# A two-layer hybrid decoder step: the order of three mixer branches and their gates

## The chip, the core and the metric

One core of a Trainium2 chip runs the whole program in one launch. The metric is the device time of one execution in microseconds (us); lower is better. Five engines run side by side, each through its own instructions in order: TensorE (PE, matrix products, with PEld for its weight loads), VectorE (DVE), ScalarE (ACT), GpSimd (POOL) and SyncE (SP, which issues most DMAs). Semaphores between them make an instruction wait for its inputs and for the buffers it overwrites.

## The reference

Two layers are applied to a prompt of 256 tokens and to 8 sample sequences of 4 tokens each, 288 columns in all, with a model width of 1024. Each layer has a mixer block, cross attention over 256 memory tokens, and a convolutional feed-forward network. The change is inside the mixer block, which is, cut to its core:

```python
h = rmsnorm(x, p['norm_mix_g'])
(q_a, k_a, v_a, x_b, y_b, q_c, k_c, v_c, r_c, a_c, g_a, g_b, g_c) = jnp.split(h @ p['w_in'], offs, axis=-1)
o_a = swa_banded(q, k, v, sink)  or  swa_step(q, k, v, k_buf, v_buf, sink)    # local attention
xc, _ = causal_dwconv(x_b, ...); hr, _ = rg_lru(xc, ...); o_b = gelu(y_b) * hr  # recurrence
o, _ = gla(q_c, k_c, v_c, log_alpha, s0); o_c = rmsnorm(o) * silu(r_c)          # linear attention
merged = (sigmoid(g_a) * (o_a @ p['w_branch_a'])
          + sigmoid(g_b) * (o_b @ p['w_branch_b'])
          + sigmoid(g_c) * (o_c @ p['w_branch_c']))
return merged @ p['w_out'], states
```

The sum over the three branches may be taken in any order.

## The kernel before

Activations lie transposed: 128 features on the partitions, 288 columns (256 of the prompt, 32 of the samples) along the free axis. Each large product takes 128x128 weight tiles against 128x288 activations, in three products of reduced-precision halves: `mm3` (L213 to L215) multiplies weight high by activation high, weight high by activation low, weight low by activation high. A weight tile of 128x1024 arrives by SP in a buffer `wst` (4 of them), ACT rounds it to `whi` (L142) and DVE subtracts to get `wlo` (L143), in 3 buffers each. A gate, an input projection or an output takes pairs of output tiles into one of two PSUM tiles `mm`; 24 products make an output tile of a gate, 48 a pair. Small steps (transposes, scores, sums over partitions) use four PSUM tiles `sm` and plain fp32 operands. Activation splits for a product are `split` (L226 to L228): ACT rounds to the high half (L227), DVE subtracts for the low half (L228).

The large products are written out in order. The small work of a layer runs in generators, called chains: `swa` (local attention), `lru` (recurrence), `gla` (linear attention), `mem_load` with `mem_rms` (the norm of the memory tokens), the norms and others. After each pair of k-steps, `proj` calls `tick`, which advances every chain whose next step is ready by an estimate: `account` adds up the time of every instruction (for an fp32 product `n / 600` us for n columns, scaled down for partial rows and columns), and a chain's `ready` is the estimated end of its last step plus 0.3 us plus whatever the generator yields. So a step's place between the large products on PE is fixed when the program is built. PE keeps the written order; the order on ACT, DVE, POOL and SP is set by a scheduler from priorities, with weights and PSUM reads put ahead.

In `swa` the prompt's blocks come first, and then the sample steps: scores of the cached keys (L643), a masked maximum on DVE (L650), exponentials on ACT (L655, L657), normalising on DVE (L659 to L666), transposes on PE (L671, L672), copies on ACT and DVE (L676, L677), the products with the values (L681, L685), a copy on ACT (L689), transposes on PE (L693), copies on ACT (L699), and the split of the sample columns, after which the branch's input `oh`, `ol` is whole. In `lru` the gates of the recurrence are eight fp32 products of 128x312 (L736), each read by a sigmoid on ACT (L737); then the chain yields until `swa` is done, and goes on with exponentials, hyperbolic tangents (L743, L744), a square root (L752), three wide passes on DVE (L747, L750, L754), a scan (L763) and a product with the gelu of the other half.

`gate(x)` makes four gate pairs of branch x (sigmoid on ACT, L1443); `branch(x)` first finishes the chain of that branch, then takes four weight tiles, multiplies each pair by its gate (DVE, L1461) and adds it to the accumulator. Branch 0 is local attention, 1 the recurrence, 2 linear attention. The order in a layer is: gates 0 and 1, branch 0, three pairs of gate 2, half of branch 1, the start of the memory chain, the last pair of gate 2, the rest of branch 1, branch 2, and then the output product `wout`, which reads the split of the accumulator that the last branch makes.

Of the kernel before, what the change touches and what calls it, by code (L numbers as in the profile page):

```python
# [19 lines left out]
KD = D // P  # L20
# [46 lines left out]
def trunk(ctx: ExitStack, tc: tile.TileContext, a: dict):  # L67
    nc = tc.nc
    V, A, PE, G = nc.vector, nc.scalar, nc.tensor, nc.gpsimd
# [78 lines left out]
    active = {}  # L148

    def account(i):  # L150

        if not hasattr(i, "engine") or not i.outs or i.opcode == "DMACopy":
            return
        e, n = str(i.engine), 1
        for _, c in i.outs[0].ap[1:]:
            n *= c
        if i.opcode == "Matmult":
            rows, cols = i.ins[0].ap[0][1], 1
            for _, c in i.ins[1].ap[1:]:
                cols *= c  # L160
            if i.ins[0].dtype == F32R:
                c = n / 2400 + 0.012
            elif getattr(i, "is_transpose", False):
                c = 0.109
            else:
                c = n / 600 * min(1.0, -(-rows // 32) / 4) * min(1.0, -(-cols // 32) / 4)
            est["pe"] += c
            if est["cur"] is not None:
                est["cur"] = max(est["cur"], est["pe"])
            return  # L170
        c = {"EngineType.DVE": 0.09 + n / 970, "EngineType.Activation": 0.12 + n / 1200}.get(e, 0.15 + n / 600)
        f = str(getattr(i, "func", "")).split(".")[-1]
        if i.opcode == "Activation" and f in TABLES and est["table"] not in TABLES[f]:
            est["table"] = TABLES[f][0]
            c += 1.28
        cur = est["cur"] if est["cur"] is not None and est["serial"] else est["pe"]
        t = est["busy"][e] = max(est["busy"].get(e, 0.0), cur) + c
        if est["cur"] is not None and not (est["serial"] and e == "EngineType.Pool"):
            est["cur"] = max(est["cur"], t + 0.1)
# [300 lines left out]
    def swa(l, got, Q, KV):  # L480
# [24 lines left out]
        for kv in range(2):  # L505
            rows = slice(kv * 64, kv * 64 + 64)
# [13 lines left out]

        yield
        pq, pg = flip(ss, 2, P), psm()
# [36 lines left out]
        for blk in range(2):  # L559
# [9 lines left out]
            for j0 in range(0, 4, hb):  # L569

                pscore = [psm(), psm()]
                for j in range(j0, j0 + hb):
                    for kv in range(2):
                        rows = slice(kv * 64, kv * 64 + 64)
# [43 lines left out]
            for kb in range(blk + 1):  # L618
                for kv in range(2):
                    rows = slice(kv * 64, kv * 64 + 64)  # L620
# [14 lines left out]
        for kv in range(2):  # L635
            rows = slice(kv * 64, kv * 64 + 64)
            G.tensor_copy(qblk[rows, :, kv, :, :], Q[rows, :, NP_:T].rearrange("p j (b s) -> p b j s", s=NS))
        yield
        pscore = psm()
# [9 lines left out]
        for g in range(2):  # L649
            V.tensor_tensor_reduce(out=pt[:, g, :], in0=pscore[:, g * 132 : g * 132 + 132], in1=cc("ms"),  # L650
                                   scale=rqs[:, g : g + 1], scalar=-3e38, op0=ALU.add, op1=ALU.max, accum_out=mx[:, g : g + 1])
        yield
        sink = prm[:, l, C_SKS : C_SKS + 1]
        V.tensor_scalar(mx, mx, sink, -1.0, ALU.max, ALU.mult)
        A.activation(es, mx, AF.Exp, bias=sink)  # L655
        for g in range(2):
            A.activation(pt[:, g, :], pt[:, g, :], AF.Exp, bias=mx[:, g : g + 1], accum_out=den[:, g : g + 1])  # L657
        yield
        V.tensor_add(den, den, es)  # L659
# [5 lines left out]
        for g in range(2):  # L665
            V.tensor_mul(pn[:, g], pt[:, g, P : P + NS].unsqueeze(1).to_broadcast([P, NB, NS]),  # L666
                         mb[:, g].unsqueeze(2).to_broadcast([P, NB, NS]))
        yield
        ptr = psm()
        for g in range(2):  # L670
            PE.transpose(ptr[:, g * P : (g + 1) * P], pt[:, g, :P], ident)  # L671
            PE.transpose(ptr[:32, (2 + g) * P : (3 + g) * P], pn[:, g].rearrange("p b s -> p (b s)"), ident)  # L672
        yield
        ptt = m1(2 * P)
        ptn = m1(2 * P)[:32]
        A.copy(ptt, ptr[:, : 2 * P])  # L676
        V.tensor_copy(ptn, ptr[:32, 2 * P : 4 * P])  # L677
        yield
        po = psm()
# [3 lines left out]
        for b in range(NB):  # L683
            r, g = 32 * (b % 4), b // 4
            PE.matmul(po[r : r + 32, g * P : (g + 1) * P], ptt[:, b * 32 : b * 32 + 32], vc[:, b, :], start=False, stop=True,  # L685
                      skip_group_check=True)
        yield
        ot = m1(2 * P)
        A.copy(ot, po[:, : 2 * P])  # L689
        yield  # L690
        po = psm()
        for g in range(2):
            PE.transpose(po[:, g * P : (g + 1) * P], ot[:, g * P : (g + 1) * P], ident)  # L693
        yield
        os = m1(P).rearrange("p (j t) -> p j t", j=4)
# [13 lines left out]
    def lru(l, got, xb, gy):  # L709
# [23 lines left out]
        for t in range(4):  # L733
            for g, (dst, c) in enumerate(((r, C_LBA), (ig, C_LBX))):
                pg = psm()
                PE.matmul(pg[:, :WO], wax[:, g * 4 + t, :], xc[:, t], start=True, stop=True)  # L736
                A.activation(dst[:, t], pg[:, :WO], AF.Sigmoid, bias=prm[:, l, c + t : c + t + 1])  # L737
            yield
        while not active["swa"].done:
            yield  # L740
# [284 lines left out]
    def mem_rms(sqs):  # L1025

        if sqs:
# [4 lines left out]
            A.copy(ss, pss[:, :NP_])  # L1032
            yield
            pt = flip(ss, 2, P)
# [315 lines left out]
    def mixers(l):  # L1350
# [84 lines left out]
        gates, acc = {}, {}  # L1435
# [13 lines left out]
        def branch(x, ms=range(0, KD, 2)):  # L1449
            oh, ol = chains[("swa", "lru", "gla")[x]].finish()  # L1450
            for m in ms:
# [8 lines left out]
                with tc.high_priority(AHEAD):  # L1460
                    V.tensor_mul(g, g, pm[:, :, :T])  # L1461
                if x:
                    (G if x == 1 or m < KD - 4 else V).tensor_add(acc[m], acc[m], g)  # L1463
                else:
                    acc[m] = g
                if x == 2:
                    w = slice(m % 4, m % 4 + 2)
                    split(bh[m // 4][:, w], bl[m // 4][:, w], acc[m])

        gate(0)  # L1470
        gate(1)
        branch(0)
        gate(2, (0, 2, 4))
        branch(1, (0, 2))
        mh = [s5v(4, NP_, F32R), s5v(4, NP_, F32R)]
        ml = [s5v(4, NP_, F32R), s5v(4, NP_, F32R)]
        mem = active["mem"] = Chain(mem_load(l, mh, ml))
        gate(2, (6,))
        branch(1, (4, 6))
        branch(2)  # L1480
        kcs = [load_kc(l, b) for b in range(NB)]
# [196 lines left out]
```

## Time and profile before

| | us |
|---|---|
| median of three runs | 1140.0 (1137.69 to 1142.15) |
| the profiled execution | 1141.05 |
| its span, from the first to the last instruction | 1139.1 |
| PE busy | 1107.9 (97%) |
| DVE busy | 794.3 (70%) |
| ACT busy | 629.8 (55%) |
| POOL busy | 252.4 (22%) |

A busy PE is not a PE at its peak: ends of matrix products are modelled, and a product at the lower clock counts as busy all the while. So the table is read together with two other views: who made PE wait, and the clock that was granted in each stretch. The stretches of which the prediction speaks lie near 40, 178 to 197 and 261 us in layer 0, and near 741 to 764 us in layer 1.

### The profile page before, as it was taken

The page shows a single profiled execution, that of the slowest core. Times are in us where ns is not written, and L with a number is a line of the kernel's source. Part 1 is how long each engine was busy: PE and PEld are TensorE (multiplying, and loading weights), DVE is VectorE, ACT ScalarE, POOL GpSimd, SP SyncE. Part 2 cuts the span into 40 slices and gives each one's busy share as a digit, 9 for nine tenths or more (in the row PEclk, how much of TensorE's full clock was granted, in tenths as well). Part 3 has the DMA queues.
Part 4 walks back from the last instruction along what each step waited for, and adds up shares of the span by engine and source line. Part 5 has one row for each costly group of instructions (what it writes and reads, how often), then busy time and mean ns, then how long its engine had stood idle before and what let it go on. Part 6 is the DMA issues. An engine that isn't in the chain of part 4 may idle for free. (4 is left out here: it accounts for less than half of the span.)

```text
span 1139.1 us, 22360 instructions
## 1 busy us (share of the span) xinstructions
PE 1107.9 (97%) x8846; PEld 1061.3 (93%) x8846; DVE 794.3 (70%) x1454; ACT 629.8 (55%) x971; POOL 252.4 (22%) x426
## 2 busy tenths in 40 slices
PE   9999997999999999999999999979999999999998
PEld 8898986999988999999999989869999899999998
DVE  6876866777765887885458769566776668878743
ACT  6545777535455656654346476864354456566532
POOL 1220101031111455550022100010311014555400
PEclk9999998999999999999999999989999999999999
DMA  8753453567466555556555435445675544455662
GB/s 279 266 181 115 152 179 116 187 201 242 150 221 234 148 167 161 155 162 197 172 170 180 138 103 178 160 141 166 203 242 166 187 142 150 167 160 158 184 193 84
DMA packets 62663, 198.11 MB, mean 174 GB/s; under 512 B 7960, under 2 KB 11768, under 8 KB 62560
## 3 DMA queue, kind: packets, MB, share of 16 engines
q1 hardware_dynamic: 59536, 188.55, 52.0%
q0 software_dynamic: 2880, 8.15, 1.9%
q8 instruction: 69, 1.13, 0.4%
q14 instruction: 34, 0.28, 0.1%
q10 hardware_dynamic: 144, 0.00, 0.0%
HBM read 187.35 MB, written 8.95 MB: 172 GB/s over the span
## 5 line engine op out<-in xcount | busy, mean ns | idle before, releaser
L142 ACT CAST whi<-wst 128x1024 fp32r<-128x1024 f32 (+1 forms) x302 | 312.5, 1036 | 302.1 <-PE mm L214 239.6
L143 DVE TENSOR_TENSOR wlo<-wst,whi 128x1024 fp32r<-128x1024 f32 (+1 forms) x302 | 373.6, 1238 | 143.1 <-ACT whi L142 141.5
L213 PE MATMUL mm<-xh,whi 128*128 128x288 f32 x1488 | 448.4, 301 | 0.0
L214 PE MATMUL mm<-xl,whi 128*128 128x288 f32 x1488 | 440.4, 296 | 1.0 <-DVE xl L264 1.0
L215 PE MATMUL mm<-xh,wlo 128*128 128x288 f32 x1488 | 439.8, 296 | 0.0
L213 PEld LDWEIGHTS mm<-xh,whi 128*128 128x128 f32 x1488 | 280.8, 189 | 12.0 <-issue 9.1
L214 PEld LDWEIGHTS mm<-xl,whi 128*128 128x128 f32 x1488 | 281.0, 189 | 2.6 <-DVE xl L264 1.9
L215 PEld LDWEIGHTS mm<-xh,wlo 128*128 128x128 f32 x1488 | 280.6, 189 | 0.4
L213 PE MATMUL mm<-s,whi 128*128 128x288 f32 (+1 forms) x756 | 226.3, 299 | 8.3 <-ACT s L227 7.4
L214 PE MATMUL mm<-s,whi 128*128 128x288 f32 (+1 forms) x756 | 225.5, 298 | 4.9 <-DVE s L228 4.9
L215 PE MATMUL mm<-s,wlo 128*128 128x288 f32 (+1 forms) x756 | 224.7, 297 | 0.0
L213 PEld LDWEIGHTS mm<-s,whi 128*128 128x128 f32 x756 | 144.8, 192 | 10.7 <-ACT s L227 7.9
L214 PEld LDWEIGHTS mm<-s,whi 128*128 128x128 f32 x756 | 145.0, 192 | 6.4 <-DVE s L228 6.3
L215 PEld LDWEIGHTS mm<-s,wlo 128*128 128x128 f32 x756 | 144.7, 191 | 0.6
L1329 DVE SCALAR_TENSOR_TENSOR y<-u,prm,y 128x304 f32<-128x304 f32 x176 | 83.6, 529 | 0.2
L1333 POOL TENSOR_TENSOR m<-y 128x256 f32<-128x256 f32 x44 | 61.0, 1386 | 70.3 <-ACT y L1330 61.3
L227 ACT CAST s<-m 128x288 fp32r<-128x288 f32 (+1 forms) x46 | 19.6, 426 | 73.7 <-POOL m L1334 73.7
L1327 ACT ACTIVATE y<-u,prm 128x304 f32<-128x304 f32 x88 | 51.9, 635 | 12.8 <-DVE u L1320 12.8
L228 DVE TENSOR_TENSOR s<-m,s 128x288 fp32r<-128x288 f32 (+1 forms) x46 | 20.7, 449 | 47.3 <-ACT s L227 47.3
L269 POOL TENSOR_TENSOR s<-s 128x288 f32<-128x288 f32 x20 | 17.7, 885 | 141.9 <-ACT s L268 141.9
L1313 POOL COPY u<-s 128x32 f32<-128x32 f32 x44 | 44.4, 1011 | 0.0
L1463 POOL TENSOR_TENSOR g<-g,g 128x576 f32<-128x576 f32 x12 | 20.9, 1738 | 79.9 <-DVE g L1461 79.9
(392 smaller groups left out, 1273.9 us busy)
## 6 DMA issues: line engine op xcount, KB each, us to landing
wst<-in_win SPq DMA_DIRECT2D x98, 512.0 KB, 3.5
wst<-in_up SPq DMA_DIRECT2D x88, 512.0 KB, 3.5
wst<-in_down SPq DMA_DIRECT2D x32, 512.0 KB, 3.7
wst<-in_wbr SPq DMA_DIRECT2D x24, 512.0 KB, 3.5
s<-in_mk SPq DMA_DIRECT2D x16, 512.0 KB, 5.6
wst<-in_wout SPq DMA_DIRECT2D x16, 512.0 KB, 4.0
wst<-in_down SPq DMA_DIRECT2D x16, 384.0 KB, 3.2
g<-in_mv SPq DMA_DIRECT2D x16, 256.0 KB, 3.3
```

The source lines that it names most:

```text
L142: A.copy(hi[:, :n], st[:, :n])
L143: (E or V).tensor_sub(lo[:, :n], st[:, :n], hi[:, :n].bitcast(F32))
L213: PE.matmul(out, wh, bh, start=first, stop=False)
L214: PE.matmul(out, wh, bl, start=False, stop=False)
L215: PE.matmul(out, wl, bh, start=False, stop=last)
L227: A.copy(hi, src)
L228: V.tensor_sub(lo, src, hi.bitcast(F32))
L1313: G.tensor_copy(us[:, :, :, 0:2], fhist[:, 2 * c : 2 * c + 2])
L1327: A.activation(y[:, i, :WFO], u[:, i, 2:], AF.Identity, scale=w[2], bias=prm[:, l, C_FCB + f : C_FCB + f + 1])
L1329: V.scalar_tensor_tensor(y[:, i, :WFO], u[:, i, j : j + WFO], w[j], y[:, i, :WFO], ALU.mult, ALU.add)
L1333: G.tensor_mul(h[:, :NP_], y[:, 0, :NP_], y[:, 1, :NP_])
L1463: (G if x == 1 or m < KD - 4 else V).tensor_add(acc[m], acc[m], g)
```

## The change

The code makes linear attention's gate and branch first, local attention's second, the recurrence's last. The accumulator therefore starts with branch 2, branch 0 adds on POOL, branch 1 adds last (POOL for the first two pairs, DVE for the other two) and makes the split for `wout`. The sample steps of `swa`, one step of its norm and one of `mem_rms` yield 1.0 instead of nothing, which puts their next step 1 us of estimated time further on. `lru` no longer yields until `swa` is done. The estimate of an fp32 product is halved (`n / 1200`), so that the estimated clock of PE advances less over small steps. No instruction of the computation is added or removed; lines after the removed wait stand two lower in the new kernel.

```diff
-                c = n / 600 * min(1.0, -(-rows // 32) / 4) * min(1.0, -(-cols // 32) / 4)
+                c = n / 1200 * min(1.0, -(-rows // 32) / 4) * min(1.0, -(-cols // 32) / 4)
...
             V.scalar_tensor_tensor(x, x, prm[:, l, g : g + 1], bc(cc(c), n), ALU.mult, ALU.mult)

-        yield
+        yield 1.0
         pq, pg = flip(ss, 2, P), psm()
...
-        yield
+        yield 1.0
         pscore = psm()
...
-        yield
+        yield 1.0
         ptr = psm()
...
-            yield
-        while not active["swa"].done:
             yield
         av, u = s5w(), s5w()
...
             A.copy(ss, pss[:, :NP_])
-            yield
+            yield 1.0
             pt = flip(ss, 2, P)
...
-                if x:
-                    (G if x == 1 or m < KD - 4 else V).tensor_add(acc[m], acc[m], g)
+                if x < 2:
+                    (G if x == 0 or m < KD - 4 else V).tensor_add(acc[m], acc[m], g)
                 else:
                     acc[m] = g
-                if x == 2:
+                if x == 1:
                     w = slice(m % 4, m % 4 + 2)
                     split(bh[m // 4][:, w], bl[m // 4][:, w], acc[m])
...
+        gate(2)
         gate(0)
-        gate(1)
-        branch(0)
-        gate(2, (0, 2, 4))
-        branch(1, (0, 2))
+        branch(2)
+        gate(1, (0, 2, 4))
+        branch(0, (0, 2))
...
-        gate(2, (6,))
-        branch(1, (4, 6))
-        branch(2)
+        gate(1, (6,))
+        branch(0, (4, 6))
+        branch(1)
```

Nine more places in the sample steps of `swa` change `yield` to `yield 1.0` in the same way, one between each pair of the steps listed above.

What this does to the order on ACT shows at three places. The first is at the start of layer 0, where ACT copies the sums of local attention's norm out of PSUM (L514, L515) and takes the logarithm of linear attention's decay (L791 to L793). Before:

```order
L788 ACTIVATE s_489<-sm_492,prm 128x288
L791 ACTIVATE s_490<-s_489 128x576
L792 ACTIVATE s_490<-s_489 128x576
L793 ACT_TABLE_LOAD
L793 ACTIVATE s_490<-s_490 128x576
L142 CAST whi_632<-wst_631 128x1024
L514 COPY m_522<-sm_515 128x256
```

And in the changed kernel, where the same lines are numbered two lower from L735 on:

```order
L786 ACTIVATE s_495<-sm_498,prm 128x288
L142 CAST whi_632<-wst_631 128x1024
L514 COPY m_522<-sm_515 128x256
L515 COPY m_523<-sm_516 32x288
L789 ACTIVATE s_496<-s_495 128x576
L790 ACTIVATE s_496<-s_496 128x576
L791 ACT_TABLE_LOAD
```

The copies for which PE waits now stand ahead of the logarithm and its table load.

The second is the end of local attention in layer 0: ACT's copies of the last transposes (L699) and the split of the sample columns (L227 from that copy), which the first product of branch 0 reads. Before:

```order
L752 ACT_TABLE_LOAD
L752 ACTIVATE s_2257<-s_2257 128x4x312
L142 CAST whi_2335<-wst_2334 128x1024
L699 COPY m_2246<-sm_2237 64x128 x2
L1443 ACT_TABLE_LOAD
L1443 ACTIVATE g_2266<-g_2266 128x2x288
L227 CAST s_848<-m_2246 128x4x32
```

And in the changed kernel:

```order
L689 COPY m_2305<-sm_2274 128x256
L747 ACTIVATE s_2231<-s_2230 128x4x312
L142 CAST whi_2433<-wst_2432 128x1024
L750 ACT_TABLE_LOAD
L750 ACTIVATE s_2231<-s_2231 128x4x312
L142 CAST whi_2470<-wst_2469 128x1024
L699 COPY m_2389<-sm_2374 64x128 x2
L227 CAST s_854<-m_2389 128x4x32
```

The split follows its copies at once, with no gate between them.

The third is ACT in layer 0 between the scores of the sample steps (L643) and the second of their exponentials (L657). In the changed kernel the sigmoids of the recurrence (L737), which stood ahead of the scores before, are mixed in:

```order
L737 ACTIVATE s_2084<-sm_2086,prm 128x312
L655 ACT_TABLE_LOAD
L655 ACTIVATE es_2081<-mx_2079,prm 128x2
L142 CAST whi_2186<-wst_2185 128x1024
L737 ACT_TABLE_LOAD
L737 ACTIVATE s_2085<-sm_2089,prm 128x312
L737 ACTIVATE s_2084<-sm_2110,prm 128x312
L737 ACTIVATE s_2085<-sm_2113,prm 128x312
L657 ACT_TABLE_LOAD
L657 ACTIVATE m_2078,den_2080<-m_2078,mx_2079 128x132
L142 CAST whi_2244<-wst_2243 128x1024
L657 ACTIVATE m_2078,den_2080<-m_2078,mx_2079 128x132
```

Three table loads now stand between the scores and the exponentials, where one stood (ahead of L655).

On PE the same small steps stand further apart. Counted in large products (L213 to L215) between them, in the order of the two programs:

| from, to | layer 0 before | after | layer 1 before | after |
|---|---|---|---|---|
| norm sums L511, L512 to their transposes L255 | 12 | 18 | 12 | 24 |
| scores L643 to transposes L671 | 60 | 66 and 8 of L736 | 60 | 72 and 4 of L736 |
| L671 to value products L681 | 18 | 36 | 18 | 60 |
| L681 to last transposes L693 | 12 | 60 | 12 | 30 |
| L693 to the first product of branch 0 | 6 | 156 | 6 | 114 |
| linear attention's last transposes (L996 before) to branch 2 | 558 | 126 | 558 | 96 |
| last L736 to the first product of branch 1 | 342 | 402 | 342 | 402 |
| memory sums L1030 to transposes L255 | 12 | 24 | none | none |

## Rows read from the trace of the kernel before

**Rows 1.** The page: busy us, share of the span, instructions of each engine.
```profile
PE 1107.9 (97%) x8846; PEld 1061.3 (93%) x8846; DVE 794.3 (70%) x1454; ACT 629.8 (55%) x971; POOL 252.4 (22%) x426
```

**Rows 2.** Waits of PE: waiting <- releaser: us in total, times, longest us.
```profile
PE mm L213 <- ACT s L227: 7.4, 2, 3.8
PE mm L214 <- DVE s L228: 4.9, 6, 1.9
PE sm L681 <- DVE m L677: 3.9, 2, 1.9
PE sm L671 <- DVE m L662: 2.6, 2, 1.3
PE sm L255 <- ACT m L1032: 1.8, 1, 1.8
PE sm L255 <- ACT m L514: 1.1, 1, 1.1
```

**Rows 3.** Timeline of PE, 177 to 199 us: start, length, operation [idle before <- releaser].
```profile
178.88 0.33 PE L671 MATMUL sm<-cst,m 128*128 128x128 f32 x1 [1.28 <-DVE m L662]
...
183.99 0.68 PE L681 MATMUL sm<-m,m 32*128 32x128 f32 x4 [1.93 <-DVE m L677]
...
191.84 0.61 PE L213 MATMUL mm<-s,whi 128*128 128x288 f32 x1 [3.82 <-ACT s L227]
193.90 0.61 PE L214 MATMUL mm<-s,whi 128*128 128x288 f32 x1 [1.45 <-DVE s L228]
```

**Rows 4.** Windows: length, busy of PE, PEld, DVE, ACT, POOL, granted clock, DMA.
```profile
43.20:46.60 3.40, 3.40 (x16) 3.40 (x16) 3.01 (x15) 1.11 (x2) 0.00 (x0) 0.50 0.97 325
190.00:196.80 6.80, 3.51 (x13) 3.19 (x14) 5.66 (x8) 1.78 (x3) 3.29 (x5) 0.50 0.23 81
261.70:265.10 3.40, 3.40 (x16) 3.40 (x15) 3.40 (x7) 1.35 (x2) 0.10 (x1) 0.50 0.81 236
746.40:749.80 3.40, 3.40 (x28) 2.76 (x27) 1.46 (x1) 2.53 (x4) 0.16 (x1) 0.50 0.67 170
756.60:763.40 6.80, 5.90 (x24) 5.90 (x25) 3.73 (x5) 1.36 (x2) 2.92 (x7) 0.50 0.56 224
200.00:206.80 6.80, 6.80 (x53) 6.80 (x52) 5.59 (x6) 4.14 (x6) 0.00 (x0) 1.00 0.67 237
```

**Rows 5.** Timeline of ACT, 169 to 193 us, its end.
```profile
189.63 1.28 ACT L1443 ACT_TABLE_LOAD   x1
190.92 0.68 ACT L1443 ACTIVATE g<-g 128x576 f32<-128x576 f32 x1
191.51 0.28 ACT L227 CAST s<-m 128x128 fp32r<-128x128 f32 x1
```

**Rows 6.** Timeline of ACT, 37 to 43 us.
```profile
38.47 1.28 ACT L793 ACT_TABLE_LOAD   x1
...
41.29 0.37 ACT L514 COPY m<-sm 128x256 f32<-128x256 f32 x1
```

**Rows 7.** Timeline of ACT, 257 to 262 us.
```profile
260.36 0.67 ACT L227 CAST s<-g 128x576 fp32r<-128x576 f32 x1 [1.33 <-DVE g L1463]
261.05 0.37 ACT L1032 COPY m<-sm 128x256 f32<-128x256 f32 x1
```

**Rows 8.** Groups of ACT, 165 to 200 us: line, operation, xcount | busy us, mean ns.
```profile
L142 ACT CAST whi<-wst 128x1024 fp32r<-128x1024 f32 x6 | 6.2, 1041 | 6.8 <-PE mm L214 6.8
...
L737 ACT ACTIVATE s<-sm,prm 128x312 f32<-128x312 f32 x5 | 2.5, 530 | 0.0
...
L657 ACT ACTIVATE m<-m,mx 128x132 f32<-128x132 f32 x2 | 0.8, 396 | 0.0
```

**Rows 9.** Timeline of PE, 158 to 160 us: one pair of the recurrence's products.
```profile
158.20 1.21 PE L736 MATMUL sm<-s,s 128*128 128x312 f32 x4
...
159.38 0.29 PE L214 MATMUL mm<-xl,whi 128*128 128x288 f32 x1
```

**Rows 10.** Waits of all engines: waiting <- releaser: us, times, longest.
```profile
ACT s L227 <- POOL s L772: 6.1, 1, 6.1
```

More of the change, by code (lines that the diff above doesn't have):

```diff
@@ L667, in swa @@
                          mb[:, g].unsqueeze(2).to_broadcast([P, NB, NS]))
-        yield
+        yield 1.0
         ptr = psm()
@@ L672, in swa @@
             PE.transpose(ptr[:32, (2 + g) * P : (3 + g) * P], pn[:, g].rearrange("p b s -> p (b s)"), ident)
-        yield
+        yield 1.0
         ptt = m1(2 * P)
@@ L677, in swa @@
         V.tensor_copy(ptn, ptr[:32, 2 * P : 4 * P])
-        yield
+        yield 1.0
         po = psm()
@@ L686, in swa @@
                       skip_group_check=True)
-        yield
+        yield 1.0
         ot = m1(2 * P)
         A.copy(ot, po[:, : 2 * P])
-        yield
+        yield 1.0
         po = psm()
@@ L693, in swa @@
             PE.transpose(po[:, g * P : (g + 1) * P], ot[:, g * P : (g + 1) * P], ident)
-        yield
+        yield 1.0
         os = m1(P).rearrange("p (j t) -> p j t", j=4)
@@ L737, in lru @@
                 A.activation(dst[:, t], pg[:, :WO], AF.Sigmoid, bias=prm[:, l, c + t : c + t + 1])
-            yield
-        while not active["swa"].done:
             yield
@@ L1032, in mem_rms @@
             A.copy(ss, pss[:, :NP_])
-            yield
+            yield 1.0
             pt = flip(ss, 2, P)
```

## The prediction

> **What bounds the kernel now.** I read the page first: PE is busy for 1107.9 us of a span of 1139.1, and no other engine passes 70% [rows 1]. So the time is PE's work, plus the time in which PE waits, plus what a lower clock takes. The change adds no product and takes none away, so only the last two can move. The waits of PE by releaser come next [rows 2]. Six of their rows matter, because they stand at steps that the change moves. The timeline of layer 0 places four of them at the end of local attention: 1.28 us before the transposes of L671, 1.93 before the value products of L681, 3.82 before the first product of branch 0 (it waits for ACT's split, L227) and 1.45 before the second (DVE's half of the split, L228) [rows 3], together 8.48. Layer 1 repeats them: 2.6 - 1.28 = 1.3, 3.9 - 1.93 = 2.0, 7.4 - 3.82 = 3.6, and the longest of L214's, 1.9 [rows 2], together 8.8. The other two are single: 1.1 us at local attention's norm near 41 us (L255 waits for the copy L514) and 1.8 at the memory's norm near 261 us (L255 waits for L1032) [rows 2]. The six make 8.48 + 8.8 + 2.9 = 20.2 us.
>
> Last I looked at the granted clock around these waits. It is 0.50, which is 1.2 GHz, in five stretches, and each lies at or just behind one of these waits [rows 4]. At full clock 53 products took 6.80 us, so 0.13 each. What the half clock took: 16 products in 3.40 us instead of 2.05 near 43 us, so 1.35; 13 in 3.51 busy us instead of 1.67 near 190 us, so 1.84; 1.35 again near 262 us; half of the 3.40 us near 746 us, where many small products are mixed in, so 1.70; 24 in 5.90 busy us instead of 3.08 near 757 us, so 2.82 [rows 4]. That is 9.1 us. **At stake are 20.2 + 9.1 = 29.3 us**, 2.6% of the time.
>
> **The end of local attention.** Each sample step needs an answer from ACT or DVE before the next can start on PE, and what hides the answer is the number of large products between. The table of distances in the section on the change gives it. A step no longer stalls when the added distance is worth more than the old wait.
> - L643 to L671: 6 products more and eight of L736 in layer 0. A pair of L736 takes from 158.20 to 159.38 less one product, 1.05 us [rows 9], so the step gains 6 x 0.13 + 4 x 1.05 = 5.0 us against a wait of 1.28. In layer 1 it is 12 x 0.13 + 2 x 1.05 = 3.7 against 1.3. The recurrence's sigmoids now stand in this gap on ACT, so I count its queue too. From the scores on, in the order shown, ACT does four sigmoids at 0.53, three rounded weight tiles at 1.04, two exponentials at 0.40 [rows 8] and three table loads at 1.28 [rows 5], which makes 9.9 us. PE comes to L671 after 66 x 0.13 + 4.2 = 12.8. About 2.9 us are left for DVE's few small steps. It fits, but not by much.
> - L671 to L681: 18 and 42 products more, 2.3 and 5.5 us, against 1.93 and 2.0. In layer 0 this is the thinnest margin, 0.4 us.
> - L693 to branch 0: 156 and 114 products instead of 6, because all or most of branch 2 and most of gate 1 come between. That is 19.5 and 14.0 us more against 5.3 and 5.5 of waiting. The split also loses what stood ahead of it: before, a table load and a gate's sigmoid ran between the copy and the split, from 189.63 to 191.51 [rows 5], and in the new order the split follows its copy.
>
> I take all 17.3 us of these waits as gone.
>
> **The two norms.** At 41 us the copy L514 started only at 41.29, because the logarithm of linear attention and its table load at 38.47 ran ahead of it [rows 6]. Now the copy stands ahead of them, and PE has 6 products (0.8 us) more as well, so the 1.1 us go. At 261 us the copy L1032 stood behind a split that waited for DVE [rows 7], and in the new order it still does. Here only distance helps: 12 products more are 1.57 us against 1.8, so 0.3 us stay.
>
> **What takes their place.** Branch 2 is now first, so linear attention must be done early: 126 and 96 products (16.4 and 12.5 us) lie between its last transposes and its branch, where 558 did. What stands between is a product on DVE and the split, near 1.2 us on each engine, so it waits for nothing. Branch 1 is last, and from the last L736 it has 402 products (52 us) where it had 342. So letting the recurrence go on without a wait for local attention is paid by nobody on PE, as far as distance goes. The accumulator's adds and the last split are as many as before, on the same engines. ACT has three table loads fewer, 40 to 37, which saves ACT 3 x 1.28 = 3.8 us [rows 5]; none of them stands on PE's path once the waits are gone, so I count them at nothing.
>
> The real unknown is branch 2's stretch. The recurrence's activations and wide DVE passes now run beside it, and its PSUM tiles must be read in turn by the same DVE. Nothing in the trace of before has these together. Bounds: nothing at the low end (in the old order the same work ran beside gates 0 and 1, and only the waits above showed), and at the high end the 12.5 us of the second rival. I take 2.5 us for both layers, near the low end: about one half-clock stretch of 1.3 and a few waits of some tenths.
>
> One rule speaks against the margins. The load of a table takes 1.28 us here, and the next activation follows at 190.92, 0.01 us after the load's end [rows 5]. The Trainium skill (ScalarE: Activation LUTs, What ACT_TABLE_LOAD costs) says that a switch costs about 1.38 us of draining beside the load. By that page three loads would put L671's input 4.1 us later, an estimate from its figure, and PE would wait for over 1 us in each layer; the trace shows no such drain here, so it stays out of the sum.
>
> **The sum.** Waits 20.2 - 0.3 = 19.9; clock 9.1; less 2.5 for what is new: 26.5 us. The profiled execution took 1141.05 us (span 1139.1), 1.05 above the median, so it would come to 1114.5, and the median to 1140.0 - 26.5 = 1113.5. I say **1114**. What the waits and the clock leave below is 1140.0 - 29.3 = 1110.7.
>
> **Rivals.**
> - *Branch 2's stretch makes new waits.* ACT takes its work in order. The last split of the recurrence waited 6.1 us there for POOL [rows 10], and nobody noticed, since PE itself stood. In the new order weight tiles for gate 1 stand behind it while PE runs at full speed, and behind the table loads too. If half of that wait reaches PE, 3 us, with one table load (1.3) and one half-clock stretch (1.9) per layer, it takes back 2 x 6.2 = 12.5 us: 1126. For it: ACT has hardly an idle moment in the third place shown. Against it: three buffers hold weights some 6 us ahead.
> - *The steps move and the waits with them.* If ACT and not the distance sets when L699 and L227 come, the waits at the end of local attention appear again at branch 0 or branch 2 and only the two norms gain: 1.1 + 1.35 + 1.5 + 1.35 = 5.3, so 1135. Against it: the split's chain ran to its end within 5.3 us of PE's arrival [rows 3], and it now has 14 us or more.
> - *Slower.* ACT becomes the bound beside branch 2. Eight table loads of layer 0 and seven of layer 1 stand between the scores and the last gates. All on PE's path they are 15 x 1.28 = 19.2 us, with the wait for POOL twice 12.2, and with as much half clock as now, 9.1: 40.5 against the gain of 29.3, so 1151. It decides from the point where ACT's arrears eat all three weight buffers; to end slower by over 0.5% it must cost 35 us, nearly all of this. Against it: ACT is busy for 55% overall [rows 1].
>
> **How the numbers follow.** A run of this kernel can tell some 0.5%, 5.7 us, from no change. My forecast has a chance of 0.68, with its own range 1110 to 1120; new waits in branch 2's stretch 0.23; the waits only moved 0.06, half of it above 1134; slower 0.03. The range of 1109 to 1128 holds nearly all of the forecast and most of the first rival. Faster by over 0.5% (below 1134.3): 0.68 + 0.23 + 0.03 = 0.94; the same 0.03; slower 0.03.
>
> **What would show it.** In the profile after, PE's rows on L227, L228 (behind local attention), L677, L662 and L514 should be gone or below 0.5 us, the wait of the memory norm near 0.3, and the granted clock 1.00 in the stretches that now have 0.50. PE's idle time should fall from 31 us to about 13. The prediction is wrong if PE waits for `whi` (L142) or `wlo` (L143) or for a gate's product (L1459, L1440) in branch 2's stretch, if L671 or L681 still waits over 1 us, or if a half-clock stretch stays where no wait is left.

## The result, and the profile after

The changed kernel takes 1111.5 us (median, 1111.13 to 1113.16), the kernel before 1140.2: a ratio of 0.9754, with an interval of 0.9742 to 0.9766. The forecast was 1114, within 1109 to 1128. The profiled execution has a span of 1109.5 us, 29.6 less than before.

Engines of the changed kernel: busy us, share of the span, instructions.
```profile
PE 1097.4 (99%) x8846; PEld 1053.7 (95%) x8846; DVE 792.9 (71%) x1454; ACT 623.6 (56%) x968; POOL 257.9 (23%) x426
```
Against [rows 1] PE does the same 8846 products in 10.5 us less, and span less busy falls from 31.2 to 12.1 us. The busy times of DVE, ACT and POOL move by 1 to 6 us.

Waits of PE in the changed kernel, its longest: waiting <- releaser: us in total, times, longest.
```profile
PE mm L214 <- DVE s L228: 1.6, 4, 0.6
...
PE mm L213 <- DVE g L1459: 0.8, 1, 0.8
...
PE mm L435 <- ACT xh L390: 0.6, 1, 0.6
PE mm L213 <- DVE g L1440: 0.5, 1, 0.5
```
Of [rows 2] the rows of L227, L677, L662, L514 and L1032 are gone; the memory's norm (L1030 now) keeps 0.2 us at its weight load (PEld), and no gap of PE. What L214 still waits for L228, and L213 for L1459, is the start of the output product in layer 1 and one place behind the mixer in each layer; all of that stood there before. Summed over the timeline, the gaps of PE are 27.7 us before and 8.6 now. (The idle times in the expectations below are this sum. Span less busy has 3.5 us more, which lie behind PE's last product.)

The stretch of local attention in layer 0, and one in layer 1: length, busy of PE, PEld, DVE, ACT, POOL, granted clock, DMA.
```profile
174.00:178.00 4.00, 4.00 (x30) 3.68 (x29) 2.46 (x8) 3.99 (x8) 0.00 (x0) 1.00 0.57 141
178.00:182.00 4.00, 4.00 (x32) 3.90 (x30) 3.33 (x4) 3.97 (x8) 0.00 (x0) 1.00 0.65 256
...
740.00:750.00 10.00, 10.00 (x87) 9.52 (x87) 9.58 (x12) 5.81 (x9) 2.40 (x3) 1.00 0.59 181
```
Where [rows 4] show 0.50 around these steps, the granted clock is 1.00 now, and PE is busy all the time. The column to notice is ACT's: 3.99 and 3.97 of 4.00 us in layer 0. ACT is full there, although the page says 56%. In layer 1 its full stretch lies ahead of the row shown: 3.94 to 3.99 of each 4.00 us from 720 to 740 us.

How much room the steps have, in layer 0: first DVE's two answers, then ACT's, then PE's three steps that read them: start, length, operation.
```profile
175.00 0.31 DVE L666 TENSOR_TENSOR pn<-m,cst 128x32 f32<-128x32 f32 x2
180.15 0.40 DVE L677 COPY m<-sm 32x256 f32<-32x256 f32 x1
```
```profile
173.24 0.18 ACT L657 ACTIVATION_READ_ACCUMULATOR m<-m,mx 128x1 f32 x1
...
188.03 0.35 ACT L689 COPY m<-sm 128x256 f32<-128x256 f32 x1
...
194.28 0.53 ACT L699 COPY m<-sm 64x128 f32<-64x128 f32 x2
194.84 0.30 ACT L227 CAST s<-m 128x128 fp32r<-128x128 f32 x1
```
```profile
176.77 0.27 PE L671 MATMUL sm<-cst,m 128*128 128x128 f32 x1
...
182.06 0.71 PE L681 MATMUL sm<-m,m 32*128 32x128 f32 x4
...
191.36 0.38 PE L693 MATMUL sm<-cst,m 128*128 128x128 f32 x2
```
The last input of the transposes (L666, which L672 reads beside L671) is there at 175.31, 1.5 us ahead of PE; L681's at 180.55, 1.5 ahead; L693's at 188.38, 3.0 ahead. None has vanished into a wait, and none has much to spare.

### The profile page after: what moved, and what is told of

Same layout as the page of the kernel before. It is cut to its first block, busy times and chain, and to the rows that moved or that the text cites. A ratio compares the mean times of both kernels' runs of the same rounds, so it can differ in the third digit from the quotient of the medians.

```text
span 1109.5 us, 22353 instructions
## 1 busy us (share of the span) xinstructions
PE 1097.4 (99%) x8846; PEld 1053.7 (95%) x8846; DVE 792.9 (71%) x1454; ACT 623.6 (56%) x968; POOL 257.9 (23%) x426
## 5 line engine op out<-in xcount | busy, mean ns | idle before, releaser
L213 PE MATMUL mm<-xh,whi 128*128 128x288 f32 x1488 | 447.8, 301 | 0.0
L214 PE MATMUL mm<-xl,whi 128*128 128x288 f32 x1488 | 439.8, 296 | 1.1 <-DVE xl L264 1.1
L215 PE MATMUL mm<-xh,wlo 128*128 128x288 f32 x1488 | 439.2, 295 | 0.0
L213 PEld LDWEIGHTS mm<-xh,whi 128*128 128x128 f32 x1488 | 280.1, 188 | 13.4 <-issue 10.2
L214 PEld LDWEIGHTS mm<-xl,whi 128*128 128x128 f32 x1488 | 280.1, 188 | 2.7 <-DVE xl L264 2.0
L215 PEld LDWEIGHTS mm<-xh,wlo 128*128 128x128 f32 x1488 | 279.8, 188 | 0.3
L213 PE MATMUL mm<-s,whi 128*128 128x288 f32 (+1 forms) x756 | 223.9, 296 | 1.4 <-DVE g L1459 0.8
L214 PE MATMUL mm<-s,whi 128*128 128x288 f32 (+1 forms) x756 | 222.8, 295 | 1.7 <-DVE s L228 1.6
L215 PE MATMUL mm<-s,wlo 128*128 128x288 f32 (+1 forms) x756 | 222.7, 295 | 0.2 <-DVE wlo L143 0.2
L213 PEld LDWEIGHTS mm<-s,whi 128*128 128x128 f32 x756 | 142.2, 188 | 4.0 <-issue 2.5
L214 PEld LDWEIGHTS mm<-s,whi 128*128 128x128 f32 x756 | 142.2, 188 | 2.9 <-DVE s L228 2.8
L215 PEld LDWEIGHTS mm<-s,wlo 128*128 128x128 f32 x756 | 142.2, 188 | 0.9 <-DVE wlo L143 0.4
L227 ACT CAST s<-m 128x288 fp32r<-128x288 f32 (+1 forms) x46 | 19.7, 427 | 73.6 <-POOL m L1332 73.6
L228 DVE TENSOR_TENSOR s<-m,s 128x288 fp32r<-128x288 f32 (+1 forms) x46 | 20.7, 451 | 47.2 <-ACT s L227 47.2
L1461 POOL TENSOR_TENSOR g<-g,g 128x576 f32<-128x576 f32 x12 | 23.2, 1930 | 50.8 <-DVE g L1459 50.8
```

The costliest lines, as they stand in the source:

```text
L213: PE.matmul(out, wh, bh, start=first, stop=False)
L214: PE.matmul(out, wh, bl, start=False, stop=False)
L215: PE.matmul(out, wl, bh, start=False, stop=last)
L227: A.copy(hi, src)
L228: V.tensor_sub(lo, src, hi.bitcast(F32))
L1461: (G if x == 0 or m < KD - 4 else V).tensor_add(acc[m], acc[m], g)
```

## The experiments

All times are medians; ratios are against the kernel before, run on the same chip. The expectations weigh the theory of the prediction, that **distance** pays (a wait is what its answer takes, less what lies between on PE, and the half clock goes with its wait), against rivals.

**1. The order alone.** Against the kernel before:
```diff
...
+        gate(2)
         gate(0)
-        gate(1)
-        branch(0)
-        gate(2, (0, 2, 4))
-        branch(1, (0, 2))
+        branch(2)
+        gate(1, (0, 2, 4))
+        branch(0, (0, 2))
...
+        branch(1)
```
The sum over the branches is changed with it, as in the change.

> The kernel before with the new order of gates and branches alone: old yields, old estimate, the recurrence still held until local attention is done. Distances on PE from L643 to L671, from L671 to L681 and at both norms stay 60, 18, 12 and 12 products; only L693 to branch 0 grows from 6 to 246 and 234. Theory D (distance: each wait is what its answer takes less what lies between on PE, and the half clock goes with its wait): the waits at branch 0 go (3.82 + 1.45 + 3.62 + 1.85 = 10.7 us) with their two half-clock stretches (1.84 + 2.82), the waits of L671 (1.28, 1.28), L681 (1.93, 1.93) and the norms (1.08, 1.84) stay, and so do the half-clock stretches near 43, 262 and 746 us: 1140.1 - 15.4 = 1124.7, PE idle 17 us. Rival Q (the split comes late because ACT's and DVE's queues are late, not because PE is near): the waits at branch 0 come back at L213 or L228 of branch 0 or 2 in some form, idle time above 22 us, 1131 or more.

Measured: 1125.7 us, ratio 0.9881 (0.9865 to 0.9898), gaps 17.3 us. PE's waits:
```profile
PE sm L681 <- DVE m L677: 3.9, 2, 1.9
PE sm L671 <- DVE m L662: 2.6, 2, 1.3
PE sm L255 <- ACT m L1032: 1.9, 1, 1.9
PE sm L255 <- ACT m L514: 0.6, 1, 0.6
```
As distance has it: of the waits whose distance is unchanged, those of L671, L681 and the memory's norm stand as they stood, to a tenth, and those at branch 0 are gone. The order alone is worth 14.4 us. Two things differ from the expectation: the first norm waits 0.6 us instead of 1.1 and no half clock follows it, and in layer 0 a half-clock stretch now follows L681, where it came only with branch 0 before (a window: length, busy of the engines, granted clock, DMA):
```profile
183.90:187.20 3.30, 3.30 (x27) 2.92 (x19) 1.46 (x1) 2.79 (x4) 0.16 (x1) 0.50 0.76 261
```

**2. The margins alone.** The changed kernel with the old order and the hold, so with the longer yields and the halved estimate only:
```diff
+        while not active["swa"].done:
+            yield
...
-        gate(2)
         gate(0)
-        branch(2)
-        gate(1, (0, 2, 4))
-        branch(0, (0, 2))
+        gate(1)
+        branch(0)
+        gate(2, (0, 2, 4))
+        branch(1, (0, 2))
...
```


> The changed kernel with the old order of gates and branches put back and the recurrence held: the longer yields and the halved estimate alone. Branch 0 now comes before local attention's steps have had their distance: L671 to L681 to L693 to branch 0 are 12, 0 and 0 products in layer 0 and 0, 0 and 0 in layer 1, where 18, 12 and 6 stood. Theory D (distance): the two norms gain 2.9 us and 2.7 of clock; the end of local attention loses what the distances lose, 18 to 26 us of waits where 17.3 were; together 1136 to 1146, most likely 1141, no gain. Rival S (the parts are separate: the margins take away the waits of L671, L681 and the norms in any order): 9.3 us of waits and 4.4 of clock go, 1126.

Measured: 1130.6 us, ratio 0.9917 (0.9902 to 0.9932), gaps 20.5. Neither theory had it: local attention still waits, but for 11.8 us, where distance said 18 to 26 and 17.3 stood before. In layer 0, the last transposes and branch 0 on PE, then ACT between them:
```profile
184.21 0.48 PE L693 MATMUL sm<-cst,m 128*128 128x128 f32 x1 [0.84 <-ACT m L689]
...
187.58 0.61 PE L213 MATMUL mm<-s,whi 128*128 128x288 f32 x1 [2.67 <-ACT s L227]
```
```profile
184.94 0.53 ACT L699 COPY m<-sm 64x128 f32<-64x128 f32 x2 [0.33 <-PE sm L693]
185.49 1.28 ACT L743 ACT_TABLE_LOAD   x1
186.78 0.56 ACT L743 ACTIVATE s<-s,sp 128x312 f32<-128x312 f32 x1
187.24 0.28 ACT L227 CAST s<-m 128x128 fp32r<-128x128 f32 x1
```
From the transposes to branch 0 it is 3.4 us here. The same transposes and ACT's copies of them in the kernel before:
```profile
186.85 0.38 PE L693 MATMUL sm<-cst,m 128*128 128x128 f32 x2
```
```profile
189.09 0.53 ACT L699 COPY m<-sm 64x128 f32<-64x128 f32 x2
```
There branch 0 started at 191.84, 5.0 us after the transposes [rows 3]: on ACT a square root with its load and a rounded weight ran until the copies at 189.09, and a load and a sigmoid between them and the split [rows 5]. So a wait is not its old length plus the distance lost: **what stands ahead of the answer on its own engine is the other half of it.** The theory was corrected for that from here on.

**3. The recurrence held.** Against the changed kernel:
```diff
+        while not active["swa"].done:
+            yield
         av, u = s5w(), s5w()
```


> The changed kernel with the recurrence held again until local attention is done. Distances at local attention are 36, 36 and 180 products in layer 0 (L671 to L681, to L693, to branch 0) where 36, 60 and 156 are in the changed kernel; in layer 1 36, 30 and 138 for 60, 30 and 114. The recurrence has at least 324 products (43 us) left to its branch. Theory D: nothing on PE pays for the hold, 1111.5, within 1.5 us either way, idle 8 to 10 us. Rival H (the recurrence has to run early, since its activations and wide passes are too long for what is left): PE waits at the first product of branch 1, 3 us or more in each layer, 1118 or more.

Measured: 1126.2 us, ratio 0.9876 (0.9862 to 0.9891), gaps 18.8. I had expected nothing, and it takes back half of the gain. Nor is it rival H as written: PE does not wait for the first product of branch 1, but within that branch and behind it.
```profile
PE mm L214 <- DVE s L228: 4.3, 4, 2.2
PE mm L213 <- DVE g L1461: 3.6, 4, 1.6
PE sm L1041 <- DVE rm L1037: 3.4, 1, 3.4
```
DVE in branch 1 of layer 0, held:
```profile
244.90 0.76 DVE L228 TENSOR_TENSOR s<-g,s 128x576 fp32r<-128x576 f32 x1 [2.04 <-ACT s L227]
245.58 0.75 DVE L1461 TENSOR_TENSOR g<-g,mm 128x576 f32<-128x576 f32 x1
246.25 0.48 DVE L1015 SCALAR_TENSOR_TENSOR s<-s,prm,s 128x256 fp32r<-128x256 f32 x1
246.64 1.21 DVE L143 TENSOR_TENSOR wlo<-wst,whi 128x1024 fp32r<-128x1024 f32 x1
247.78 0.75 DVE L1463 TENSOR_TENSOR g<-g,g 128x576 f32<-128x576 f32 x1
```
and in the changed kernel, where the same lines are numbered two lower:
```profile
243.93 0.76 DVE L228 TENSOR_TENSOR s<-g,s 128x576 fp32r<-128x576 f32 x1 [2.04 <-ACT s L227]
244.60 0.75 DVE L1459 TENSOR_TENSOR g<-g,mm 128x576 f32<-128x576 f32 x1
245.39 0.76 DVE L1461 TENSOR_TENSOR g<-g,g 128x576 f32<-128x576 f32 x1
246.06 1.22 DVE L143 TENSOR_TENSOR wlo<-wst,whi 128x1024 fp32r<-128x1024 f32 x1
```
L1015 is the memory's load. Its second half stood ahead of branch 1; with the hold it is written between the splits of the sum, where DVE has its weights, products, sums and splits back to back, and what follows comes later: the sum stands at 247.78 (L1463) where it stood at 245.39 (L1461). Experiments 5 and 6 tell apart whether the hold or the memory costs.

**4. The old estimate.**
```diff
-                c = n / 1200 * min(1.0, -(-rows // 32) / 4) * min(1.0, -(-cols // 32) / 4)
+                c = n / 600 * min(1.0, -(-rows // 32) / 4) * min(1.0, -(-cols // 32) / 4)
```


> The changed kernel with the old estimate of fp32 products (n / 600). Distances at local attention are 42, 30 and 108 products in layer 0 and 42, 30 and 108 in layer 1, from L643 to L671 156; at the norms 18 and 24 as in the changed kernel. But ACT's order at the first norm is the old one: the logarithm and its table load stand ahead of the copy L514. Theory D: no wait in local attention; at the first norm 1.08 - 6 x 0.13 = 0.3 us stays, with or without its half clock of 1.35: 1111.8 to 1113.2. Rival E (the estimate is what spreads local attention's steps): waits of L671 or L681 of 1 us or more in each layer come back, 1115 or more.

Measured: 1112.3 us, ratio 0.9757 (0.9743 to 0.9772), gaps 9.5. No wait in local attention, 0.6 us at the first norm, no half clock. With the other parts there, the halved estimate is worth about 1 us (1112.3 against 1111.5).

**5. The memory later, no hold.** Against the changed kernel:
```diff
-        mh = [s5v(4, NP_, F32R), s5v(4, NP_, F32R)]
-        ml = [s5v(4, NP_, F32R), s5v(4, NP_, F32R)]
-        mem = active["mem"] = Chain(mem_load(l, mh, ml))
         gate(1, (6,))
         branch(0, (4, 6))
+        mh = [s5v(4, NP_, F32R), s5v(4, NP_, F32R)]
+        ml = [s5v(4, NP_, F32R), s5v(4, NP_, F32R)]
+        mem = active["mem"] = Chain(mem_load(l, mh, ml))
```


> The changed kernel, recurrence not held, with the memory chain started one half branch later: behind branch(0, (4, 6)) instead of behind branch(0, (0, 2)). In the run with the recurrence held, the second half of the memory's load (eight passes of L1014, L1015 in each layer, the square and POOL's sum in layer 0) had moved to between the splits of the accumulator in branch 1, and PE waited there. Theory T (branch 1 is where DVE has no room: per weight tile of 24 products, 3.2 us, it does a low half of 1.22 and product, sum or split of 0.75 each, so whatever else is put there comes out as PE's wait): the same waits come without any hold, 8 to 14 us: 1120 to 1126. Rival H (it is the hold of the recurrence itself, its late gelu product and split): without the hold nothing comes back, 1111.5 to 1113.

Measured: 1124.3 us, ratio 0.9849 (0.9829 to 0.9868), gaps 17.8. The waits of experiment 3 are back without a hold:
```profile
PE mm L214 <- DVE s L228: 5.1, 4, 2.3
PE mm L213 <- DVE g L1459: 3.7, 4, 1.6
PE mm L213 <- ACT s L227: 2.1, 2, 1.1
```

**6. The hold, and the memory earlier.** Against the changed kernel, the hold of experiment 3 and:
```diff
+        mh = [s5v(4, NP_, F32R), s5v(4, NP_, F32R)]
+        ml = [s5v(4, NP_, F32R), s5v(4, NP_, F32R)]
+        mem = active["mem"] = Chain(mem_load(l, mh, ml))
         branch(0, (0, 2))
-        mh = [s5v(4, NP_, F32R), s5v(4, NP_, F32R)]
-        ml = [s5v(4, NP_, F32R), s5v(4, NP_, F32R)]
-        mem = active["mem"] = Chain(mem_load(l, mh, ml))
         gate(1, (6,))
```


> The changed kernel with the recurrence held, and the memory chain started half a branch earlier, ahead of branch(0, (0, 2)). All of the memory's load then stands ahead of the splits of branch 1 again, and only the copy of its norm between them, as in the changed kernel. Theory T (what costs is the memory's work in branch 1, the hold only pushed it there): 1111.5 to 1114.5, PE idle 8 to 11 us. Rival H (the hold itself costs): as with the hold alone, 1124 to 1127.

Measured: 1110.4 us, ratio 0.9730 (0.9710 to 0.9749), gaps 7.3. With 5 this settles it: beside the new margins the hold itself costs nothing, and the memory's work in branch 1 costs 13 to 16 us (1124.3 and 1126.2, against 1111.5 and 1110.4). Why the hold moves that work is read from the code alone: the chains share one estimated clock, and what the recurrence does later pushes the memory's next step.

**7. The order without the hold.** The kernel before with the order of experiment 1, and:
```diff
-        while not active["swa"].done:
-            yield
         av, u = s5w(), s5w()
```


> The kernel before with the new order and without the hold, and with the old yields and the old estimate. Local attention's distances are then 156, 36, 18 and 126 products in layer 0 (L643 to L671, to L681, to L693, to branch 0), without any longer yield, because the recurrence's steps now share the estimated time with local attention's. Theory D: the waits of L671 and L681 go here too; only the two norms keep 12 products: 0.63 near 42 us and 1.91 with 1.35 of half clock near 255 us, as in the run with the new order alone: 1111.5 + 3.9 = 1115.4, PE idle 11 to 12 us. Rival Y (the longer yields are what local attention needs): L671 and L681 wait 1 us or more in each layer, 1119 or more.

Measured: 1116.1 us, ratio 0.9777 (0.9755 to 0.9799), gaps 11.7:
```profile
PE sm L255 <- ACT m L1030: 1.9, 1, 1.9
PE sm L681 <- DVE m L677: 0.8, 2, 0.4
PE sm L255 <- ACT m L514: 0.7, 1, 0.7
```
As distance has it, with two waits of 0.4 at L681 more. Neither the longer yields nor the new estimate is needed to spread local attention, once the recurrence's steps share its estimated time.

**8. More work for ACT.** Against the changed kernel (the estimate leaves these passes out; they change no output):
```diff
         for t in range(4):
...
+            for _ in range(6):
+                A.activation(u[:, t], r[:, t], AF.Exp, scale=sp8[:, l, t : t + 1])
...
             A.activation(av[:, t], r[:, t], AF.Exp, scale=sp8[:, l, t : t + 1])
```


> The changed kernel with 24 more exponentials of 128x312 in each layer's recurrence on ACT, written to a tile that is overwritten afterwards; the outputs are the same, and the estimate does not count them, so that PE's written order stays. One takes 0.45 us from start to start, so 10.8 us per layer. In the changed kernel ACT has no idle time from 174 to 190 us, and the copy L689 is done 3.0 us before PE comes to L693 (188.4 against 191.4). Theory A (the slower rival's mechanism: ACT is full there, and what is added to it beyond some 3 us comes out as PE's wait, at L693 or at a rounded weight): 7 us of waits in each layer and 1.5 to 3 of half clock with each: 1128 to 1132. Rival B (three buffers of weights and ACT's 56% leave room): under 3 us in all, 1111 to 1114.5.

Measured: 1132.7 us, ratio 0.9923 (0.9904 to 0.9943), gaps 26.1. ACT's copy, PE's step that reads it, and a window between, in layer 0:
```profile
200.34 0.35 ACT L689 COPY m<-sm 128x256 f32<-128x256 f32 x1
```
```profile
200.75 0.47 PE L693 MATMUL sm<-cst,m 128*128 128x128 f32 x1 [8.55 <-ACT m L689]
```
```profile
194.00:198.00 4.00, 0.00 (x0) 0.00 (x0) 0.00 (x0) 4.00 (x9) 0.00 (x0) 0.93 0.41 131
```
The copy comes 12.3 us later than in the changed kernel and PE waits 8.55; layer 1 waits 8.75, at L681. Of the 12.3 us, 0.7 are a later start of everything in this profile: PE and ACT both run 0.68 us behind the changed kernel before the first added pass (L671 at 177.45 against 176.77). The other 11.6 less 8.55 leave a room of about 3 us in layer 0, the 3.0 that the rows above gave for L693: the slower rival's mechanism is real, and not far off.

**9. Plain yields.** Against the changed kernel, at the eleven places that yield 1.0 (the section on the change speaks of nine beside the four that its diff shows; there are seven):
```diff
-            yield 1.0
+            yield
```


> The changed kernel with all the longer yields taken back; the new order, the halved estimate and the missing hold stay. Distances at local attention are 54 products and six of L736, 24, 48 and 156 in layer 0, 60 and six of L736, 24, 48 and 120 in layer 1; at the norms 12, 18 and, for the memory, 12. On ACT the copy L514 stays ahead of the logarithm. Theory D: the memory's norm waits 1.9 us again with 1.35 of half clock, L681 waits some 0.5 us in each layer as in the run with the order and without the hold (18 more products there than before gave 0.45), the first norm nothing or 0.3: 1111.5 + 4.3 = 1115.8, between 1114.5 and 1117. Rival Y (the longer yields carry local attention): L671 and L681 each over 1 us in each layer with their half clock, 1119 or more.

Measured: 1118.6 us (1117.09 to 1119.94), ratio 0.9806 (0.9793 to 0.9820). The profile is of an execution of 1117.1 us, gaps 13.1:
```profile
PE sm L681 <- DVE m L677: 2.1, 2, 1.6
...
PE sm L255 <- ACT m L1030: 0.9, 1, 0.9
...
PE mm L215 <- DVE wlo L143: 0.7, 1, 0.7
...
PE sm L693 <- ACT m L689: 0.7, 1, 0.7
```
Slower than I expected and faster than rival Y, and otherwise spread: the memory's norm waits half of what I gave it, L681 three times as much in layer 0, and small waits come at L693, at a weight's low half and elsewhere. No half-clock stretch follows any of them in this profile. The two executions that took 2.4 and 2.9 us more have a mean granted clock of 0.998, the two faster ones 1.000; so half clock is part of their loss, and in which stretch isn't shown. The yields are worth 6 to 7 us, and in which wait they pay hangs on the other parts.

**10 to 12. The changed kernel beside two that may be better.** Number 12 is the kernel of experiment 6. Number 10 is the same, with the second pair's sum of branch 1 on DVE:
```diff
-                    (G if x == 0 or m < KD - 4 else V).tensor_add(acc[m], acc[m], g)
+                    (G if x == 0 or m < KD - 6 else V).tensor_add(acc[m], acc[m], g)
```


> The changed kernel itself, as the measure for the other kernels of this call: 1111.5, PE idle 8.6 us.

> The kernel with the recurrence held and the memory chain started ahead of branch(0, (0, 2)) again, now beside the changed kernel on one chip. In the first run PE's idle time was 7.3 us where the changed kernel had 8.6 (no wait of 0.54 for a gate's product in layer 1, none of 0.64 near the program's start). Theory T: 0.5 to 1.5 us below the changed kernel. Rival N (the difference was that run's): within 0.4 us.

> The changed kernel with the recurrence held and the memory chain started ahead of branch(0, (0, 2)), and in branch 1 the sum of the second pair on DVE instead of POOL (POOL takes 2.29 us there, and DVE stands 2.04 us behind it, waiting for ACT's split). Theory T: the split of the second pair comes 1 us earlier, and of layer 1's three waits at the start of the output product (0.80, 0.54, 0.40) the first goes: 0.8 to 1.5 us below the same kernel without this edit. Rival F (DVE is full in branch 1, 0.75 us more of work there cancels it): within 0.4 us of it, or above.

Measured: the changed kernel 1112.3 us (1111.33 to 1112.44), ratio 0.9750 (0.9736 to 0.9763); number 12 1110.2 (1109.84 to 1110.75), 0.9733 (0.9720 to 0.9747); number 10 1109.8 (1109.38 to 1110.31), 0.9729 (0.9716 to 0.9742). Side by side no execution of either is as slow as the fastest of the changed kernel, so the hold with the memory started earlier is worth about 2 us more (0.2%); the earlier start without the hold was not run. Of number 10's edit rival F holds: the wait of 0.8 goes and small ones of 0.3 to 0.4 come, gaps 7.5 and 7.5.

## Why the prediction was right, point by point

Put side by side:

| kernel | us | gaps of PE, us |
|---|---|---|
| before | 1140.2 | 27.7 |
| margins alone (2) | 1130.6 | 20.5 |
| order and margins, recurrence held (3) | 1126.2 | 18.8 |
| order alone (1) | 1125.7 | 17.3 |
| order, recurrence not held (7) | 1116.1 | 11.7 |
| all but the longer yields (9) | 1118.6 | 13.1 |
| all but the new estimate (4) | 1112.3 | 9.5 |
| the change | 1111.5 | 8.6 |
| the change, held, memory earlier (6) | 1110.4 | 7.3 |

*The waits.* The sum said 20.2 us at stake and 19.9 gone. All of them are gone as gaps of PE (20.1 by the timeline). Experiment 1 shows that they hang on the distances one by one: of those left as they were, all but the first norm wait as they did.

*The clock.* I worked out 9.1 us from five stretches; PE's busy time fell by 10.5, and no stretch but the end is at half clock. The term was 1.4 short, and by what is not shown. The two products behind a wait that [rows 3] show at 0.61 us, where 0.29 is usual, lie inside the window of 190 us that I had counted. One candidate is the product ahead of a gap: it counts as busy for its whole 0.29 us, where a product in a row adds 0.13, and ten such gaps are gone.

*What takes their place.* I allowed 2.5 us; the gaps that are new come to 8.6 - (27.7 - 20.1) = 1.0 us. The largest wait among them is 0.64 us near the program's start (L435, away from the mixer); the next is a gate's product (0.54, L1440) in layer 1's branch 2. By the letter of what I had called a sign of being wrong, this one occurred; it cost half a microsecond, and no half clock came with it. The wait for POOL on which the first rival leans is there too, 2.9 us at the recurrence's last split in layer 1, and PE is busy throughout it (3.00 us of 3.00 from 749.40 to 752.40). (I had written that PE itself stood during the old one of 6.1 us; from 755.10 to 761.40 it was busy for 4.30 of 6.30.) The two sizes, clock and new gaps, are 1.4 and 1.5 us, and both err to the same side: the span fell by 29.6 us where the sum said 26.5. Part of that is not in the medians, which lie 28.7 apart and end 2.5 below the forecast.

*The margins.* For L671 I had left 2.9 us for DVE's small steps; they end 1.9 us after ACT's last step (173.42 to 175.31), and 1.5 are left: 3.4 in all, so that piece holds. L681 had 1.5 us to spare where I counted 0.4. I had taken its latency as fixed: before, 5.1 us passed from L671 to L681 with PE waiting at the end (178.88 to 183.99) [rows 3], and in the changed kernel the answer is there 3.8 us after L671 (176.77 to 180.55). Experiment 2 shows another latency that moved with what stands ahead on ACT. The memory's norm kept no gap of PE; I said 0.3.

*The table loads.* By the rule of the Trainium skill that I set against the margins (ScalarE: Activation LUTs, What ACT_TABLE_LOAD costs), L671 would wait for over 1 us, by my estimate. It doesn't wait, and in experiment 2 the activation behind a load starts at 186.78, 0.01 us after the load's end. Where the page and this trace differ, the trace decides.

*The recurrence's hold.* "Paid by nobody on PE" is true and was half of the matter. I looked for what going on costs, and not for what holding would have cost beside the new margins: 14.7 us, by way of the memory's load (3, 5, 6). That part of the change is what lets order and margins add up: 14.4 and 9.5 us apart, 13.9 together while the hold stands, 28.7 without it. Beside the old margins the hold costs 9.6 us in another way (1 against 7): there it keeps local attention's distances short. The same sum for the change less this one part would have been wrong by some 12 us (1114 against 1126.2).

*The slower rival.* I held ACT's 55% against it. That is an average over the whole span; in the stretch that matters ACT is full, and experiment 8 puts the point from which PE waits at some 3 us of added work in layer 0, not at three weight buffers. The price was right in kind: 10.8 us more on ACT cost 8.55 and 8.75 us of waits. The chance I gave it (0.03) was low for a room of 3 us. (In layer 1 the trace has six table loads behind the scores, not the seven that I counted; that is 1.3 us of the price of 40.5.)

*The waits only moved.* That did not happen here; it is what experiment 9 shows without the longer yields, in small.

## What to carry to other kernels

Read a wait as two halves, the work between the steps on the engine that waits and the queue ahead of the answer on the engine that answers; a reordering changes both. Weigh an engine by its busy share in the stretch where the steps stand, never by the page's average, and measure the room by adding work to it. When parts of a change share one planned clock, try each part taken away from the whole, not only each part alone: the line that seems free may be the one that keeps some other chain out of the way.

## What the runs showed of the hardware that I had not expected

**DVE's low half and POOL's sum shut each other out.** Two passes of each in the changed kernel, in layer 0, DVE first:
```profile
232.94 2.34 DVE L143 TENSOR_TENSOR wlo<-wst,whi 128x1024 fp32r<-128x1024 f32 x1 [0.24 <-ACT whi L142]
...
236.09 1.23 DVE L143 TENSOR_TENSOR wlo<-wst,whi 128x1024 fp32r<-128x1024 f32 x1
```
```profile
232.78 1.42 POOL L1461 TENSOR_TENSOR g<-g,g 128x576 f32<-128x576 f32 x1 [0.20 <-DVE g L1459]
236.10 2.50 POOL L1461 TENSOR_TENSOR g<-g,g 128x576 f32<-128x576 f32 x1 [1.89 <-DVE g L1459]
```
POOL starts first at 232.78 and takes 1.42 us; DVE's low half, 1.22 us elsewhere, takes 2.34 and ends 1.08 us after POOL. At 236.09 DVE starts first and takes 1.23; POOL's sum takes 2.50 and ends 1.28 after it. In both pairs the one that comes second stands for the rest of the other's pass. The Trainium skill (SBUF — State Buffer, Who interferes with whom) says the same, that the two share a port pair as an exclusive lock; this trace agrees. It is not why number 10's sum on DVE cost nothing: in number 12 the sum that it moves starts on POOL behind DVE's low half (240.97 against 240.75 us in layer 0) and takes 2.28 us, and the low half keeps its 1.22. But DVE then sits idle for 2.03 us until ACT's split of that sum, and the sum takes 0.76 us on DVE.

**A wait's length does not tell what it costs in clock.** The 1.93 us before L681 in experiment 1 and the 1.08 near 41 us of the kernel before were followed by a stretch at 0.50. The same 1.93 in layer 0 of the kernel before was not, until the next wait [rows 3, 4]; nor was the 1.28 before L671, there or in experiment 1, nor the 1.63 before L681 in experiment 9, though in experiment 2 a wait of 1.65 before the same step was (from 181.78 on). So I would take the clock's share from the rows of the stretch, as the prediction did, and from no rule on the wait.
